# Encoder layer on one core: the third gate traced two products later, plain weights behind h's splits, other tiles for the sums of h, and scratch placed ahead of its rings

## The chip, the cores and the metric

The kernel runs on one core of a Trainium2 chip. The metric is the device time of one execution in microseconds (us). A profile of one execution is shown beside the times of several others.

## The reference

One layer of a hybrid encoder over 512 tokens of width 2048, in float32:

```python
h = rms_norm(x, pre_mix_g)
z = h @ w_in                                  # q, k, v (1024 each) and u (1024)
a = chunked_attention(q, k, v, rel_bias)      # 8 heads of 128, chunks of 64, 8 chunks back
p = multiscale_pool(u, pool_w, pool_scale)    # trailing means over 2, 4, 8, 16 tokens
x = x + rms_norm(concat(a, p) @ w_o, post_mix_g)
h = rms_norm(x, pre_ffn_g)
up = causal_dwconv(h @ w_up, conv_w, conv_b)  # w_up: 2048 x 11264, 3 taps
y = (gelu(up[:, :5632]) * up[:, 5632:]) @ w_down
x = x + rms_norm(y, post_ffn_g)
```

## The kernel before

**Products.** TensorE works on a rounded type, so each factor is split into a high part (rounded by ACT, L140) and a low part (the rest, subtracted by DVE, L141), and a product is the sum of two or three products of parts. The large products are also cut by a seven-product scheme: halves of both factors are added or subtracted, product i (1 to 7) is formed of such sums, and the results are combined. Products 5, 6 and 3 use sums of the left factor. Products 1, 6, 7 and 4 of a block add up in one PSUM bank (`qa`), 5 and 3 in another (`qg`), 2 in a third (`qd`). Products 6, 7 and 4 are "turned": the narrow matmuls with the low part (L176) come first, the wide ones with the high part (L170) second. One such product of the up projection is eight wide and eight narrow matmuls.

**Up projection.** It is done in 44 column blocks of 256 (block `PLAIN + k`; an even one feeds the gelu, the next odd one is multiplied by it). The first two blocks are plain (`plain`, three products of parts, no seven-product scheme); the other 42 are numbered k = 0 to 41. `Factors.order` is a hand-written order of pairs (k, i): the first eight are products 1 and 2 of blocks 0 to 3, then the plain blocks, then blocks 0 to 3 with spacing five, and from block 4 on with spacing seven. Around the places that matter here the order is

- (2,7), (3,3), (2,4), (3,6), (4,1), (3,7), (4,2), (3,4), (4,5), (4,3), (5,1), (4,6), ...
- at the end (41,5), (40,6), (41,3), (41,1), (40,7), (41,6), (40,4), (41,7), (41,2), (41,4).

`seven(k, i)` first calls `factors.get()`, which prepares the factor four products ahead (`AHEAD`): a split into two slots of the ring `w4` (eight slots, `wfh`, `wfl`), and behind it, on POOL, an accumulating load (L1110) that turns the raw block in place into the next sum that is needed. Then it issues the matmuls. `keep(k, i)` moves results out of PSUM: L1416 copies the bank of 5, L1421 the bank of 1, 6 after product 6, L1427 after 7. After product 4 `keep_all(k)` puts the block z together (L1435 to L1438). Then `gate(u, z)` (for even blocks) applies the three convolution taps (L1310 on ACT, L1311 and L1312 on DVE, for two halves) and the gelu (L1333) into the second half of the tile `zc`; `product(u, ...)` (odd blocks) applies the taps to its own z, multiplies into the same half (L1343), and stores the result to DRAM from it (L1346, POOL). z itself is the first half of `zc`.

**h.** Before that, h is transposed in eight pairs (`turn_back`; pairs 0 to 3 by `turn(0, 1)` and `turn(2, 3)`, the others between the groups of the first plain block) and split into the tiles `gT`. `h_sums` forms the sums for products 5, 6 and 3, each as two halves of 8 KB, in the tiles h0 to h5 of the pool `ps`, which held other data before.

**Down projection.** The seven-product scheme again, in five blocks of the inner dimension (CU = 4 up blocks each). Left factors (`ah`, `al`) are split from `gc` (loaded from DRAM) or from `s` in `scratch`; right factors (`bh`, `bl`) are split from `t` or `b`; for three of the first right factors the split lies ready in DRAM (`rw01`, `rw11`, `rw02`, each `h` and `l`) and is loaded by POOL (L1214). The first left factor `a` is split into two slots of `w4`. Two products with it come first (`pa`), then the product `pd` with `rw02` and the first `ah`. The pool `pr` lies over the tiles of `ps`: its `wh` and `wl` tiles take `rw01` and `rw11`. The pool `p4` lies over the pools of the up projection; its rings stand one behind the other in the order of the loop `for r in (...): r("place")`: among them `slot_h` (eight slots of 4 KB for `ah`), `slot_l` (eight for `al`) and `scratch` (one of 4 KB). In the version before, the first slot of `slot_h` lies exactly over the first slot of `w4`, `scratch` over the small tiles of the pool `p3`. A tile that lies over another is free to be written as soon as what used the other tile is done.

**Order.** TensorE's instructions stay in the order of the program. Those of the other engines are placed by a planner, which issues what it holds for ready and uses the place in the program as a priority. `tc.issue_after(ins)` adds an edge: what is traced in the block is issued behind `ins` on `ins`'s engine. Each engine then runs its own queue in order.

Of the kernel before, what the change touches and what calls it, by code (L numbers as in the profile page):

```python
# [81 lines left out]
def encoder_layer(ctx: ExitStack, tc: tile.TileContext, x, xT, vecs, rel, post_mix, post_ffn,  # L82
# [23 lines left out]
    def bank(name):  # L106
        return psum.tile([P, 512], F32, tag="ps", name=name)
# [30 lines left out]
    def split(hi, lo, src, scale=None):  # L138
        if scale is None:
            rounded = nc.scalar.activation(hi, src, AF.Copy)  # L140
            rest = nc.vector.tensor_sub(lo, src, f32(hi))  # L141
        else:
            rounded = nc.scalar.activation(hi, src, AF.Copy, scale=scale)
            rest = nc.vector.scalar_tensor_tensor(lo, src, scale, f32(hi), op0=ALU.mult, op1=ALU.subtract)
        split.last, split.rest = rounded.ins, rest.ins
        return rounded.ins
# [213 lines left out]
    for kb in range(KD):  # L360
        i, o = divmod(kb, 8)
# [259 lines left out]
    with tc.tile_pool(name="p1", bufs=2, reuse_waits="tile") as p1:  # L621
# [90 lines left out]
        def turn(h):  # L712
            probs = [state.pop(("p", h, t)) for t in range(NT)]
            pts = [bank(f"pt{h}_{k}") for k in range(3)]
            pts = [pts[0], pts[1][:, P:], pts[2][:, 2 * P:], pts[1][:, :P]]
            for k in (0, 1, 3, 2):
                for t in range(k, NT):
                    nc.tensor.transpose(pts[k][:, (t - k) * P:(t - k + 1) * P],
                                        probs[t][:, k * P:(k + 1) * P], ident)
            for k in range(NT):  # L720
                n, at = S - k * P, PT_AT[k] + k * P - PT_Q[k]
                split(pth[:, at:at + n], ptl[:, at:at + n], pts[k])
# [179 lines left out]
    if True:  # L902
# [56 lines left out]
        a22 = wo_left("a22", 1, 1, [acc8(f"a22{p}", "A", F32R).rearrange("p (a b) -> p a b", a=8) for p in "hl"])  # L959
# [189 lines left out]
        factors = Factors()  # L1149
# [33 lines left out]
    later, turns = {}, {}  # L1183
# [122 lines left out]
    if True:  # L1306
# [16 lines left out]
        def new_z():  # L1323
            return two(holder("zc")[0])

        def gate(u, z):
            if u == NU - 1:
                a = raw1("ca")[:, :2, :]
            else:
                a = two(holder("zc")[1])  # L1330
            for j in range(2):
                taps(z[:, j, :], 2 * u + j, a[:, j, :])
            nc.scalar.activation(flat(a), flat(a), AF.Gelu_apprx_tanh)  # L1333
            return a

        def product(u, g, z):
            for j in range(2):
                if u == NU - 1 and j:
                    c = raw_x("cx")[:, :S]
                else:  # L1340
                    c = holder("m8")[0]
                taps(z[:, j, :], KF + 2 * u + j, c)
                nc.vector.tensor_mul(g[:, j, :], g[:, j, :], c)  # L1343
            if u < NC * CU:
                for i in range(2):
                    nc.gpsimd.dma_start(gd[u // CU][i][:, u % CU, :, :], g[:, :, i * H:(i + 1) * H])  # L1346
            elif u < NU - 1:
                nc.gpsimd.dma_start(gd_last[u - NC * CU], g)
            else:
                product.last = g  # L1350
# [23 lines left out]
        def h_sums():  # L1374
            def keep(n, i, at, v):
                hs.setdefault(n, {})[i] = h8(at, f"h{n}{i}", F32R).rearrange("p (a b c) -> p a b c", a=4, b=2)
                split(*(hs[n][i][:, :, p, :] for p in range(2)), v)

            halves = [[wholes[k, t][:, 4 * i:4 * i + 4, :] for k in range(2) for t in range(2)] for i in range(2)]
            for i, (a11, a21, a12, a22) in enumerate(halves):  # L1380
                nc.vector.tensor_sub(a22, a22, a21)
                keep(5, i, (4, 1)[i], a22)
                nc.vector.tensor_sub(a21, a11, a21)
                nc.vector.scalar_tensor_tensor(a22, a22, -1.0, a11, op0=ALU.mult, op1=ALU.subtract)
                keep(6, i, (0, 5)[i], a22)
            for a11, a21, a12, a22 in halves:
                nc.vector.scalar_tensor_tensor(a12, a22, -1.0, a12, op0=ALU.mult, op1=ALU.subtract)
            for i in range(2):
                keep(3, i, (3, 2)[i], halves[i][2])
            return [v[1] for v in halves]  # L1390

        banks, gates = {}, {}

        zs = {}
# [7 lines left out]
        def keep(k, i):  # L1402

            if i == 1:
                v = zs[k, "1"] = first_parts[:, k % 4, :]
                nc.scalar.activation(v, banks[k, "a"][:, :T], AF.Copy)
                nc.vector.tensor_add(v, banks[k, "a"][:, T:], v)
            elif i == 2:
                v, d = zs[k, "1"], banks.pop((k, "d"))
                nc.vector.tensor_add(v, d[:, :T], v)  # L1410
                nc.vector.tensor_add(v, d[:, T:], v)
            elif i in (5, 3) and k < 4:
                return
            elif i == 5:
                zs[k, "5"] = raw_x("zb")[:, :S] if k == end else holder("m8")[1]
                nc.scalar.activation(zs[k, "5"], banks[k, "g"], AF.Copy)  # L1416
            elif i == 6:
                m = raw_x("zm") if k == end else holder("m8")[2]
                zs[k, "m"] = m.rearrange("p (a b c) -> p a b c", a=2, b=2)
                v = wide(zs[k, "m"][:, :1])  # L1420
                nc.scalar.activation(v, banks[k, "a"], AF.Copy)  # L1421
                nc.vector.tensor_add(v, banks[k, "g"] if k < 4 else banks.pop((k, "g")), v)
                if k < 4:
                    nc.vector.tensor_add(v, banks.pop((k, "e")), v)
            elif i == 7:
                v = wide(zs[k, "m"][:, 1:])
                nc.scalar.activation(v, banks[k, "a"], AF.Copy)  # L1427
                nc.vector.tensor_add(v, banks.pop((k, "g")) if k < 4 else zs.pop((k, "5")), v)
            elif i == 4:
                keep_all(k)  # L1430

        def keep_all(k):
            one, m, a = zs.pop((k, "1")), zs.pop((k, "m")), banks.pop((k, "a"))
            z = new_z()
            nc.scalar.activation(z[:, 0, :T], one, AF.Copy)  # L1435
            nc.vector.tensor_add(z[:, 1].rearrange("p (a b) -> p a b", a=2), m[:, :, 0], m[:, :, 1])
            nc.scalar.activation(z[:, 0, T:], a[:, T:], AF.Copy)
            nc.vector.tensor_add(z[:, 0, T:], a[:, :T], z[:, 0, T:])  # L1438
            u, p = divmod(PLAIN + k, 2)
            if p:  # L1440
                product(u, gates.pop(u), z)
            else:
                gates[u] = gate(u, z)

# [19 lines left out]
        def start(k, i):  # L1464
            seven(k, i)
            keep(k, i)
# [5 lines left out]
        for k, i in factors.order[:7]:  # L1472
            start(k, i)
        turn(0, 1)
        start(3, 2)
        turn(2, 3)
        factors.open = True
        def plain(p, behind):
            ups = [bank(f"up{p}_{j}") for j in range(2)]
            for q in range(4):  # L1480
                factors.used += 1
                factors.prefetch(0)
                factors.prefetch(factors.AHEAD if p else (2, 2, 3, factors.AHEAD)[q])
                w = weights.get(f"w{p}0_{q}", 0)
                for kb in range(4 * q, 4 * q + 4):
                    for j in range(2):
                        mm3(ups[j], part(w, j, slice(kb % 4 * P, (kb % 4 + 1) * P)), g_both(hT, kb),
                            kb == 0, kb == KD - 1)
                behind(q)
            return ups  # L1490
# [24 lines left out]
        for k, i in factors.order[8 + 4 * PLAIN:]:  # L1515
            seven(k, i)
            keep(k, i)
            if (k, i) == (end, 6):
                summed.close()
                pr = ctx.enter_context(tc.tile_pool(name="pr", bufs=2, side="right", reuse_waits="tile"))  # L1520
            if (k, i) == (end, 6):
                next_first()
            elif (k, i) == (end - 1, 4):
                next_first()
# [5 lines left out]
    with tc.tile_pool(name="p4", bufs=2, reuse_waits="tile") as p4:  # L1530
# [3 lines left out]
        raw2 = later["raw2"] = ring("raw2", (CU, S), 2)  # L1534
        half_g = ring("g", (CU, 2, H), 2)
        slot_h, slot_l = ring("ah", (CU, H), 8), ring("al", (CU, H), 8)
        scratch = ring("scratch", (CU, H), 1)
        product_part = later["part"] = ring("part", (2, S), 5)
# [2 lines left out]

        for r in (product_part, later["wh"], half_g, later["raw1"], raw2, later["wl"], slot_h, slot_l, scratch):
            r("place")
        half_g("place")
        for _ in range(3):
# [230 lines left out]
```

## Time and profile before

| | |
|---|---|
| times of three runs | 1865.05, 1865.7, 1866.84 us |
| median | 1865.7 us |
| profiled execution | 1864.49 us, span 1862.6 us |
| mean granted clock of TensorE | 0.998 |
| TensorE busy | 1840.5 us, 9514 matmuls |
| DVE, ACT, POOL busy | 1484.1, 1100.1, 306.8 us |

The span runs from the first to the last instruction of the profiled execution. A row of the timeline gives the start, the duration, the engine, the line in the kernel, the operation, what it writes and reads, and in square brackets how long the engine had been idle before it and what ended that. A row of the waits gives the engine and line that waited, what it waited for, the total in us, how often, and the longest. PE is TensorE.

### The profile page before, as it was taken

What the parts mean: (1) busy time and instruction counts of PE and PEld (TensorE: products, weight loads), DVE (VectorE), ACT (ScalarE), POOL (GpSimd) and SP (SyncE); (2) the same over time, 40 slices, a digit from 0 to 9 for tenths busy, and PEclk for the clock granted to TensorE, in tenths of its full rate; (3) what the DMA queues carried; (4) which work ended last, traced back from release to release, by engine and by line L of the source; (5) the groups of instructions that cost most, each with busy time, mean ns of one, the idle gap of its engine ahead of it and who ended that gap; (6) DMA issues with size and microseconds to landing.
All of it is one profiled execution on the core that took longest, in us unless ns stands there. A gap on an engine that the chain in (4) does not pass through costs nothing.

```text
span 1862.6 us, 25315 instructions
## 1 busy us (share of the span) xinstructions
PE 1840.5 (99%) x9514; PEld 1579.1 (85%) x9514; DVE 1484.1 (80%) x1776; ACT 1100.1 (59%) x1438; POOL 306.8 (16%) x407
## 2 busy tenths in 40 slices
PE   9999999999999989999999999999999999999998
PEld 7888888888888878888888888888888888888886
DVE  6988778888678777777787777777776899899876
ACT  7655455456586655665666665666655665565553
POOL 3411001100001212212212122121121001111101
PEclk9999999999999999999999999999999999999999
DMA  8599977998979878998988888899888977777785
GB/s 319 176 317 300 323 228 228 271 275 313 328 270 293 200 172 192 206 208 199 200 201 206 207 200 199 202 206 204 203 177 280 354 228 173 196 207 179 175 241 148
DMA packets 139547, 428.63 MB, mean 230 GB/s; under 512 B 12001, under 2 KB 15457, under 8 KB 133729
## 3 DMA queue, kind: packets, MB, share of 16 engines
q0 software_dynamic: 55440, 175.66, 46.9%
q1 hardware_dynamic: 83984, 251.36, 38.2%
q8 instruction: 75, 1.23, 0.3%
q14 instruction: 48, 0.39, 0.1%
HBM read 372.97 MB, written 104.33 MB: 256 GB/s over the span
## 4 chain that ended last, share of the span: by engine, by line
PE 65%; DMA 2%; issue 1%; DVE 1%; ACT 0%; POOL 0%; POOLq 0%; DVEq 0%; ACTq 0%
PE qa L170 15%; PE qa L176 8%; PE qg L170 8%; PE qg L176 4%; PE pa L162 4%; PE pa L164 4%; PE pa L165 4%; PE qd L170 4%; PE pg L162 2%; PE pg L164 2%; PE pg L165 2%; PE qd L176 2%; DMA bl<-rw02l 1%; PE pd L164 1%; PE pd L165 1%
## 5 line engine op out<-in xcount | busy, mean ns | idle before, releaser
L170 PE MATMUL qa<-gT,wfh 128*128 128x512 f32 x1176 | 294.6, 392 | 0.0
L141 DVE TENSOR_TENSOR wfl<-x,wfh 128x1024 fp32r<-128x1024 f32 x161 | 197.2, 1225 | 88.3 <-ACT wfh L140 83.8
L170 PEld LDWEIGHTS qa<-gT,wfh 128*128 128x128 f32 x1176 | 211.6, 189 | 37.9
L140 ACT ACTIVATE wfh<-x 128x1024 fp32r<-128x1024 f32 x161 | 170.3, 1058 | 97.4 <-PE qg L170 47.2
L1110 POOL DMA_DIRECT2D x<-in_w_up x122 | 104.7, 858 | 462.8 <-DVE wfl L141 438.3
L176 PE MATMUL qa<-gT,wfl 128*128 128x256 f32 x1176 | 164.7, 283 | 2.2 <-ACT m L1421 2.1
L170 PE MATMUL qg<-h,wfh 128*128 128x512 f32 x640 | 159.5, 392 | 5.5 <-ACT m L1416 5.5
L176 PEld LDWEIGHTS qa<-gT,wfl 128*128 128x128 f32 x1176 | 154.7, 191 | 6.8 <-ACT m L1421 2.3
L170 PEld LDWEIGHTS qg<-h,wfh 128*128 128x128 f32 x640 | 121.0, 189 | 30.9 <-ACT m L1416 5.7
L141 DVE TENSOR_TENSOR bl<-b,bh 128x2048 fp32r<-128x2048 f32 x56 | 127.2, 2288 | 18.6 <-ACT bh L140 11.7
L140 ACT ACTIVATE wfh<-wy 128x1024 fp32r<-128x1024 f32 x98 | 103.4, 1055 | 64.6 <-PE qd L170 49.0
L140 ACT ACTIVATE bh<-b 128x2048 fp32r<-128x2048 f32 x56 | 106.1, 1913 | 57.1 <-DVE b L1230 23.3
L141 DVE TENSOR_TENSOR wfl<-wy,wfh 128x1024 fp32r<-128x1024 f32 x98 | 119.5, 1219 | 10.5 <-ACT wfh L140 6.9
L162 PE MATMUL pa<-bh,ah 128*128 128x512 f32 x320 | 124.5, 389 | 0.0
L164 PE MATMUL pa<-bl,ah 128*128 128x512 f32 x320 | 124.5, 389 | 0.0
L165 PE MATMUL pa<-bh,al 128*128 128x512 f32 x320 | 124.5, 389 | 0.0
L170 PE MATMUL qd<-gT,wfh 128*128 128x512 f32 x392 | 97.0, 390 | 0.0
L176 PEld LDWEIGHTS qg<-h,wfl 128*128 128x128 f32 x640 | 87.3, 190 | 6.2
L176 PE MATMUL qg<-h,wfl 128*128 128x256 f32 x640 | 89.2, 282 | 0.0
L170 PEld LDWEIGHTS qd<-gT,wfh 128*128 128x128 f32 x392 | 73.2, 188 | 15.0
L170 PE MATMUL qa<-h,wfh 128*128 128x512 f32 x336 | 84.1, 392 | 0.0
L141 DVE TENSOR_TENSOR wfl<-wz,wfh 128x1024 fp32r<-128x1024 f32 x49 | 60.0, 1224 | 28.5 <-PE qa L170 25.3
(574 smaller groups left out, 4340.6 us busy)
## 6 DMA issues: line engine op xcount, KB each, us to landing
x<-in_w_up POOLq DMA_DIRECT2D x122, 512.0 KB, 5.9
b<-in_w_down SPq DMA_DIRECT2D x32, 1024.0 KB, 6.8
wt<-in_w_o POOLq DMA_DIRECT2D x24, 1024.0 KB, 14.7
wz<-in_w_up SPq DMA_DIRECT2D x42, 512.0 KB, 5.1
x<-in_w_up SPq DMA_DIRECT2D x42, 512.0 KB, 5.0
wy<-in_w_up SPq DMA_DIRECT2D x42, 512.0 KB, 3.8
wy<-in_w_up POOLq DMA_DIRECT2D x42, 512.0 KB, 6.0
sum<-part POOLq DMA_DIRECT2D x38, 512.0 KB, 6.2
```

Of the source, the lines that this page charges most:

```text
L140: rounded = nc.scalar.activation(hi, src, AF.Copy)
L141: rest = nc.vector.tensor_sub(lo, src, f32(hi))
L162: nc.tensor.matmul(ps, l[0], r[0], start=first, stop=False, skip_group_check=onto)
L164: nc.tensor.matmul(low, l[0], r[1], start=False, stop=False, skip_group_check=onto)
L165: nc.tensor.matmul(ps, l[1], r[0], start=False, stop=last, skip_group_check=onto)
L170: nc.tensor.matmul(ps, w[0][:, kb], pairs[kb][0], start=fresh and not kb, stop=last, skip_group_check=not fresh)
L176: nc.tensor.matmul(ps[:, sl], w[1][:, kb], pair[:, sl], start=False, stop=last, skip_group_check=not fresh)
L1110: nc.gpsimd.dma_start(self.raw[k, what], self.block(k, m, kh), accum_op=ALU.add)
```

## The change

- In `h_sums` the halves of sum 5 go to h1 and h0 (before: h4 and h1), the first half of sum 6 to h4 (before: h0). The second half of sum 6 and sum 3 stay.
- `keep_all(2)` no longer calls `gate` for block 2 (u = 2, the third gate). It keeps u and z, and the loop calls `gate` after product (4,1) and its `keep`, two products after (2,4).
- In the first plain block the factor preparation is cut from two ahead to one in the first group, and what is prepared in the first two groups gets edges behind the splits of h after `turn(0, 1)` and `turn(2, 3)`, on ACT and on DVE.
- In `p4` `scratch` is placed ahead of `slot_h` and `slot_l`, so both rings lie 4 KB further on.

```diff
-                keep(5, i, (4, 1)[i], a22)
+                keep(5, i, (1, 0)[i], a22)
 ...
-                keep(6, i, (0, 5)[i], a22)
+                keep(6, i, (4, 5)[i], a22)
 ...
             if p:
                 product(u, gates.pop(u), z)
+            elif k == 2:
+                zs["late"] = u, z
             else:
                 gates[u] = gate(u, z)
 ...
         turn(0, 1)
+        behind_h = [(split.last, split.rest)]
         start(3, 2)
         turn(2, 3)
+        behind_h.append((split.last, split.rest))
 ...
                 factors.prefetch(0)
-                factors.prefetch(factors.AHEAD if p else (2, 2, 3, factors.AHEAD)[q])
+                with ExitStack() as behind_split:
+                    for ins in behind_h[q] if not p and q < 2 else ():
+                        behind_split.enter_context(tc.issue_after(ins))
+                    factors.prefetch(factors.AHEAD if p else (1, 2, 3, factors.AHEAD)[q])
 ...
             keep(k, i)
+            if (k, i) == (4, 1):
+                u, z = zs.pop("late")
+                gates[u] = gate(u, z)
 ...
-        for r in (product_part, later["wh"], half_g, later["raw1"], raw2, later["wl"], slot_h, slot_l, scratch):
+        for r in (product_part, later["wh"], half_g, later["raw1"], raw2, later["wl"], scratch, slot_h, slot_l):
             r("place")
```

## The prediction

> **What bounds the kernel now.** First the page and the waits of TensorE, to see how much can be won at all.
>
> ```profile
> span 1862.6 us, 25315 instructions
> PE 1840.5 (99%) x9514; PEld 1579.1 (85%) x9514; DVE 1484.1 (80%) x1776; ACT 1100.1 (59%) x1438; POOL 306.8 (16%) x407
> ...
> PE qg L170 <- ACT m L1416: 5.5, 1, 5.5
> PE qa L176 <- ACT m L1421: 2.1, 1, 2.1
> PE up L164 <- DVE gT L141: 1.6, 1, 1.6
> PE pd L164 <- DMA bl<-rw02l: 1.5, 1, 1.5
> PE pd L162 <- ACT ah L140: 1.1, 1, 1.1
> ```
>
> TensorE is busy for 99% of the span, and no matmul is added or removed. What the change can win is the list of waits. The first five rows come to 11.8 us and sit at three places, near 575, 673 to 692, and 1438 us; each part of the change lies ahead of one of them. So I read the three places in the timelines of the engines. The profiled execution took 1864.49 us, 1.9 around its span; the median shown, 1865.7, is 1.2 above it. A TensorE gap that closes comes off either one whole.
>
> **Plain weights behind h's splits.** The view is the timeline: start, duration, engine, line, idle time and what ended it.
>
> ```profile
> 573.01 0.48 PE L162 MATMUL up<-gT,w_0h 128*128 128x512 f32 x1
> 575.05 0.51 PE L164 MATMUL up<-gT,w_0h 128*128 128x512 f32 x1 [1.56 <-DVE gT L141]
> 581.20 0.48 PE L162 MATMUL up<-gT,w_1h 128*128 128x512 f32 x1
> 570.47 1.08 ACT L140 ACTIVATE w_2h<-w_2r 128x1024 fp32r<-128x1024 f32 x1
> 571.42 1.07 ACT L140 ACTIVATE gT<-a 128x1024 fp32r<-128x1024 f32 x1
> 571.50 1.22 DVE L141 TENSOR_TENSOR w_1l<-w_1r,w_1h 128x1024 fp32r<-128x1024 f32 x1
> 572.63 1.22 DVE L141 TENSOR_TENSOR w_2l<-w_2r,w_2h 128x1024 fp32r<-128x1024 f32 x1
> 573.77 1.22 DVE L141 TENSOR_TENSOR gT<-a,gT 128x1024 fp32r<-128x1024 f32 x1
> ```
>
> The second matmul of plain product 0 needs the low half of gT, whose subtraction stands behind w_1l and w_2l on DVE and whose rounding stands behind w_2h on ACT. The issue_after edges force the opposite order on both engines. ACT then rounds gT at 570.5 instead of 571.4 and is done by 571.5; DVE is free at 571.50 and finishes the low half at 572.8. TensorE asks for it at 575.05 - 1.56 = 573.5. The wait goes: 1.56 us. What is pushed back is w_1l, to about 572.8 to 574.0, and w_2 and w_3, to behind the second split, about 579. w_1 is first read at 581.20, w_2 and w_3 later still, so their cover is 7 us. Queues: the next weights' loads on SP wait for raw slots that free up to 4 us later. They are for the second plain product, sixteen matmul groups on, so I cost that at nothing. Bounds: 0 (the planner puts other DVE work into the hole) to 1.56; I take 1.56, because an edge, unlike a priority, cannot be jumped.
>
> **The third gate.**
>
> ```profile
> 675.46 1.21 PE L176 MATMUL qa<-gT,wfl 128*128 128x256 f32 x8 [2.13 <-ACT m L1421]
> 684.25 1.98 PE L170 MATMUL qg<-h,wfh 128*128 128x512 f32 x8
> 692.71 3.41 PE L170 MATMUL qg<-h,wfh 128*128 128x512 f32 x8 [5.54 <-ACT m L1416]
> 673.41 1.52 ACT L1310 ACTIVATE zc<-zc,vec 128x512 f32<-128x512 f32 x2 [3.58 <-DMA gd<-zc]
> 674.83 0.58 ACT L1421 ACTIVATE m<-qa 128x512 f32<-128x512 f32 x1
> 676.90 0.42 ACT L1435 ACTIVATE zc<-first_parts 128x256 f32<-128x256 f32 x1 [0.54 <-DVE zc L1312]
> 677.22 0.36 ACT L1406 ACTIVATE first_parts<-qa 128x256 f32<-128x256 f32 x1
> 687.74 1.06 ACT L140 ACTIVATE wfh<-x 128x1024 fp32r<-128x1024 f32 x1 [5.48 <-DMA x<-in_w_up]
> 674.25 0.75 DVE L1311 SCALAR_TENSOR_TENSOR zc<-zc,vec 128x511 f32<-128x511 f32 x1 [4.83 <-ACT zc L1310]
> 674.92 1.22 DVE L141 TENSOR_TENSOR wfl<-x,wfh 128x1024 fp32r<-128x1024 f32 x1
> 679.24 1.22 DVE L141 TENSOR_TENSOR wfl<-x,wfh 128x1024 fp32r<-128x1024 f32 x1
> 680.76 0.91 POOL L1110 DMA_DIRECT2D x<-in_w_up  x1 [13.19 <-DVE wfl L141]
> ```
>
> One stall makes both gaps. The gate's two taps (L1310) overwrite the tile that product 1 is still storing, so ACT stands 3.58 us for the store; L1421, queued behind them, holds up the matmuls at 675.46. DVE stands 4.83 us with it, the low half at 679.24 comes late, the accumulating load of x leaves POOL at 680.76, ACT waits 5.48 us for it and goes on at 687.74, 7.0 us after the issue, and L1416 (the copy of (4,5)'s bank), behind that, holds up product (4,3) until 692.71, another 4.97 us.
>
> Does tracing the gate later move the taps behind L1421? I think not. The planner places what is ready and uses the trace position only between ready ones: L1435 at 676.90 belongs to keep_all(3), traced after product (3,4), and stands ahead of L1406 at 677.22, which is traced three products earlier. And on DVE the first tap's L1311 stands ahead of the low half at 674.92, whose slot is free only when the last matmul of (3,6) has read it. So in the plan the first tap on ACT was over before (3,6) ended, when L1421 cannot have been ready. A later trace position does not hold it back, and the wait of 2.13 us stays.
>
> What does change is who goes first on DVE when several are ready. L1422, L1424 and the low half of (4,5) now outrank the gate's remaining taps. The second pair, L1311 and L1312 (0.67 us each from start to start, as between the DVE rows at 674.25 and 674.92), falls behind that low half, which starts 1.3 us earlier, and so do POOL's load, its landing, and (4,3). The gap shrinks from 5.54 to 4.2 us. The gelu comes up to 2.7 us later; the 5.48 us that ACT idles ahead of 687.74 hide it.
>
> The gap has a second price. Eight wide matmuls last 1.98 us at 684.25 and 3.41 after the gap, at 692.71: 1.43 us more. The stretches show why; the column after the engines is the granted clock.
>
> ```profile
> 675.50:678.50 3.00, 3.00 (x17) 2.67 (x18) 3.00 (x5) 1.55 (x3) 0.00 (x0) 1.00 0.39 102
> 687.20:692.70 5.50, 0.00 (x0) 0.00 (x0) 2.96 (x4) 3.57 (x5) 0.85 (x1) 0.95 0.89 154
> 692.70:695.70 3.00, 2.99 (x7) 2.39 (x8) 2.12 (x4) 1.23 (x2) 0.00 (x0) 0.53 0.97 193
> ```
>
> After the 2.13 us gap the clock is 1.00; after 5.54 it is 0.53. A mean of 0.95 over 5.5 idle us, if it fell to one half once, puts the fall 0.55 us before their end (0.05 x 5.5 / 0.5), 5.0 us after the last matmul. A gap of 4.2 us ends before that, so I take the 1.43 as saved too. Together 2.7 us; bounds 0 and 8.5 (2.13, all of 5.54 but the 0.6 that a copy like L1421 takes in any case, and 1.43).
>
> The Trainium skill, page "TensorE: Matmul & The Clock Gate", Part 1, says the clock goes to half after an idle window of about 3.4 us, counted by windows that run free of the kernel. By that rule read strictly, 4.2 us is still too long, the 1.43 us stays, and the whole sum below becomes 5.5 instead of 6.9, or 1860.2 us. The trace agrees on the half clock (0.53 after 5.54 us) and shows no gap between 2.13 and 5.54 us.
>
> **Tiles of h's sums, and scratch ahead of its rings.** These act together at the last change of stage.
>
> ```profile
> 1404.26 1.98 PE L170 MATMUL qg<-h,wfh 128*128 128x512 f32 x8
> 1438.76 0.49 PE L162 MATMUL pd<-bh,ah 128*128 128x512 f32 x1 [1.15 <-ACT ah L140]
> 1440.72 0.50 PE L164 MATMUL pd<-bl,ah 128*128 128x512 f32 x1 [1.48 <-DMA bl<-rw02l]
> 1437.65 1.06 ACT L140 ACTIVATE ah<-gc 128x1024 fp32r<-128x1024 f32 x1 [8.99 <-PE pa L165]
> 1406.04 0.86 POOL L1110 DMA_DIRECT2D x<-in_w_up  x1 [7.50 <-DVE wfl L141]
> 1414.97 0.55 POOL L1214 DMA_DIRECT2D bh<-rw01h  x1 [7.51 <-PE qa L170]
> x<-in_w_up POOLq DMA_DIRECT2D x1, 512.0 KB, 5.4
> bh<-rw01h POOLq DMA_DIRECT2D x1, 1024.0 KB, 5.7
> bl<-rw11l POOLq DMA_DIRECT2D x1, 1024.0 KB, 14.3
> bl<-rw02l POOLq DMA_DIRECT2D x1, 1024.0 KB, 18.7
> ```
>
> Six loads of 1 MB leave POOL, rw01, rw11 and rw02, each a high and a low half, the first four from 1414.97 on. The first lands in the first tile of the old sums, which held half of sum 6, read by (41,6) until then; the other three queue behind it. They land 5.7 to 14.3 us after issue, about 2.9 us per MB, and push rw02l, issued near 1422.0 (1440.7 less 18.7), to 1440.7. Now that tile holds half of sum 5, last read by (41,5), two products of 2.79 us before (41,3) and so over at 1401.5; the next load's tile held half of sum 3, read until (41,3), begun at 1404.26, ends at 1407. So rw01h leaves near 1402 and the other three near 1407.5, behind the x load of 1406.04. All four are in by about 1420, and rw02l lands at its own price and one MB more, 8.6 to 11.5 us (one or two MB at 2.9 us on top of 5.7), near 1432. TensorE asks for it at 1437.6, where its wait for ah begins. Moved past on POOL: the x load for (41,4). It lands 5.4 us after 1406.04, and the rounding of it is not due before the slot frees at about 1413.8, so 2 us are in hand.
>
> That alone leaves 1.15: ACT's rounding of ah stood 8.99 us for the last matmul on the first a. Its slot, the ring's first or second, lies over the low half of that a. With scratch ahead the rings start 4 KB later, so it lies over a factor of one of the last products ((41,7), four after (41,3), ends at 1421.0 and (41,4) at 1426.6), and the rounding follows the landing of gc instead. Scratch now lies on a's slot and is free from 1437.4; the product that needs it starts two products of 5.4 us after that, so that costs nothing. Either part alone leaves a gap (the slot alone the whole 2.6, the tiles alone about 1.1); together 2.63 goes. Bounds 0 and 2.63. What is late next is the factors of the following products, whose loads also land earlier. In h_sums itself the new tiles are free long before their writes: nothing.
>
> **Sum.** 1.56 + 2.7 + 2.63 = 6.9 us: 1864.5 less 6.9 is 1857.6 for the profiled execution, 1858.8 for the median.
>
> **Rivals.**
> - The gate does move behind L1421 and the low half of (4,5). For: the taps may be a near tie in the plan. Against: the two orders above. Then 2.13 goes; the low half follows (4,1)'s last read, 673.3, and the x load leaves at about 674.9; with the same 7.0 and 4.97 (4,3) starts at 686.9, where TensorE is free at 687.2 - 2.13 = 685.0: a gap of 1.9 and no half clock. 2.13 + 3.64 + 1.43 = 7.2 instead of 2.7: 11.4 in all, 1854.3.
> - The end or the plain weights give nothing because the planner fills the hole or picks another slot, or the gate gives nothing: 1860.4 to 1863, taken as 1861.7.
> - Slower: POOL takes the rw loads ahead of the x load of (41,4). Three MB at 2.9 us in front of it and 5.4 for itself from about 1409 put it at 1423.1; ACT's rounding (1.06) and L1421 (0.58) of (41,6) follow, and (41,7) starts at 1424.8 instead of 1418.2: 6.6 us, and 1.43 for the clock. 1865.7 + 8.0 - 6.9 = 1866.8; with only the end's 2.63 won beside it, 1871.1. It decides once that load lands after 1416.5. Against: it leaves at 1406.04, a microsecond before the second rw load's tile is free.
>
> **How the numbers follow.** Forecast 0.49 (1857.5 to 1860.5, the clock's 1.43 included), the moving gate 0.19, a part that gives nothing 0.22, slower 0.10. The predicted time is the forecast's, 1858.8. The range 1853.8 to 1863.5 takes in the moving gate and most of the failed parts, and leaves out about 2 in 10. 0.2% is 3.7 us, about what a measurement can tell here: faster needs less than 1862.0. Forecast and moving gate give that with nearly all of 0.68, the failed parts with a third: 0.74. Same 0.20, slower 0.06.
>
> **What would show it.** Right: no wait of up on gT; L1310 still ahead of L1421 with a wait for gd, the wait of qa near 2.1 and of qg near 4.2 at full clock; rw01h issued near 1402, no wait of pd on rw02l or ah. Wrong: L1310 behind L1421; rw01h still after 1414; a new TensorE wait between 1405 and 1425 on L1421, or after 1448 on the next factors.

## The result, and the profile after

The changed kernel takes 1857.36 us (median of 5 runs, 1855.83 to 1857.90), the kernel before 1866.84 us on the same chip (5 runs, 1865.05 to 1867.86). The ratio is 0.995, 95% interval 0.9935 to 0.9965, so the gain is 9.5 us, between 6.5 and 12.1. The forecast was 1858.8 us and a gain of 6.9. The profiled execution took 1857.87 us. Its span is 6.6 us shorter than that of the first profile of before.

The two longest waits of TensorE in the changed kernel (us in total, times, longest); its span is 1856.0 us.

```profile
PE qa L176 <- ACT m L1421: 3.1, 1, 3.1
PE qg L170 <- ACT m L1416: 1.2, 1, 1.2
```

Three of the five waits of before are gone: that of up on gT and the two of pd. The other two changed places in size: the one ahead of (3,7), on L1421, grew from 2.1 to 3.1 us, and the one ahead of (4,3), on L1416, fell from 5.5 to 1.2. Among the shorter waits one is new, 0.9 us for DVE at L742, near 346 us. It lies far ahead of what the change touches, and f0, the same kernel run again below, does not show it.

The timeline of the changed kernel at plain product 0, the stretch where the wait of 1.56 us stood:

```profile
573.49 0.47 PE L162 MATMUL up<-gT,w_0h 128*128 128x512 f32 x1
573.81 0.39 PE L164 MATMUL up<-gT,w_0h 128*128 128x512 f32 x1
571.14 1.06 ACT L140 ACTIVATE gT<-a 128x1024 fp32r<-128x1024 f32 x1
572.11 1.04 ACT L140 ACTIVATE w_1h<-w_1r 128x1024 fp32r<-128x1024 f32 x1
572.23 1.23 DVE L141 TENSOR_TENSOR gT<-a,gT 128x1024 fp32r<-128x1024 f32 x1
```

gT's rounding now stands ahead of w_1's on ACT, its low half is done at 573.46 (572.23 + 1.23), and the second matmul, at 573.81, follows the first with no idle time. The half is ready 0.35 us ahead, where the forecast had 0.7 (572.8 against 573.5).

The timeline of the changed kernel around the third gate:

```profile
675.20 2.08 PE L176 MATMUL qa<-gT,wfl 128*128 128x256 f32 x8 [3.08 <-ACT m L1421]
690.58 2.12 PE L170 MATMUL qg<-h,wfh 128*128 128x512 f32 x8 [1.22 <-ACT m L1416]
673.15 1.52 ACT L1310 ACTIVATE zc<-zc,vec 128x512 f32<-128x512 f32 x2 [4.53 <-DMA gd<-zc]
674.57 0.57 ACT L1421 ACTIVATE m<-qa 128x512 f32<-128x512 f32 x1
677.66 1.22 DVE L141 TENSOR_TENSOR wfl<-x,wfh 128x1024 fp32r<-128x1024 f32 x1
679.12 0.74 DVE L1311 SCALAR_TENSOR_TENSOR zc<-zc,vec 128x511 f32<-128x511 f32 x1
664.86 1.49 POOL L1346 DMA_DIRECT2D gd<-zc  x2 [1.01 <-DVE zc L1343]
679.18 0.91 POOL L1110 DMA_DIRECT2D x<-in_w_up  x1 [12.83 <-DVE wfl L141]
```

ACT still takes the taps (L1310) ahead of the copy L1421 and stands for the store of gd. On DVE the low half of (4,5) at 677.66 now stands ahead of the second tap pair. The load of x leaves POOL 6.03 us after the taps begin (679.18 - 673.15). Before it was 7.35 (680.76 - 673.41): 1.32 us less.

The same place by stretches; the clock is the number after the busy times of the engines.

```profile
670.99:674.40 3.41, 1.13 (x9) 0.90 (x7) 0.40 (x1) 1.25 (x2) 0.00 (x0) 1.00 0.49 199
674.40:677.81 3.41, 2.61 (x10) 2.51 (x11) 3.41 (x6) 2.54 (x6) 0.00 (x0) 0.50 0.24 65
677.81:681.23 3.42, 3.42 (x9) 2.65 (x9) 2.50 (x4) 1.29 (x2) 0.91 (x1) 0.50 0.36 108
```

The clock is at one half for 6.83 us, from 2.3 us into the gap ahead of (3,7) onwards. TensorE works 2.61 + 3.42 us of it, and at full speed that work takes half as long: 3.0 us lost, where the first profile of before lost 1.4 us behind its second gap.

The end, in the timeline of the changed kernel:

```profile
1402.62 0.86 POOL L1110 DMA_DIRECT2D x<-in_w_up  x1 [7.50 <-DVE wfl L141]
1403.91 0.67 POOL L1214 DMA_DIRECT2D bh<-rw01h  x1
1418.56 0.54 POOL L1214 DMA_DIRECT2D bl<-rw02l  x1
1430.51 1.06 ACT L140 ACTIVATE ah<-gc 128x1024 fp32r<-128x1024 f32 x1 [5.28 <-DMA gc<-gd]
1434.25 0.39 PE L164 MATMUL pd<-bl,ah 128*128 128x512 f32 x1
```

and the last load in its list of DMA issues (KB, us to landing):

```profile
bl<-rw02l POOLq DMA_DIRECT2D x1, 1024.0 KB, 14.0
```

rw01h leaves right behind the load of x, and ah's rounding follows the landing of gc, no longer the last matmul on a. rw02l lands at 1432.6 (1418.56 + 14.0), 1.7 us before its first reader.

### The profile page after: what moved, and what is told of

Its sections match the earlier page's. It is cut to its first block, busy times and chain, and to the rows that moved or that the text cites. A ratio compares the mean times of both kernels' runs of the same rounds, so it can differ in the third digit from the quotient of the medians.

```text
span 1856.0 us, 25317 instructions
## 1 busy us (share of the span) xinstructions
PE 1840.9 (99%) x9514; PEld 1580.5 (85%) x9514; DVE 1484.0 (80%) x1776; ACT 1099.0 (59%) x1438; POOL 306.5 (17%) x407
## 3 DMA queue, kind: packets, MB, share of 16 engines
q8 instruction: 75, 1.23, 0.3%
## 4 chain that ended last, share of the span: by engine, by line
PE 95%; DMA 2%; DVE 1%; issue 1%; ACT 0%; SPq 0%; POOL 0%; POOLq 0%; DVEq 0%; ACTq 0%
PE qa L170 19%; PE qa L176 10%; PE qg L170 9%; PE qd L170 5%; PE qg L176 5%; PE pa L165 4%; PE pa L164 4%; PE pa L162 4%; PE m L162 3%; PE m L164 3%; PE m L165 3%; PE qd L176 3%; PE pg L165 2%; PE pg L164 2%; PE pg L162 2%; PE v L164 2%
## 5 line engine op out<-in xcount | busy, mean ns | idle before, releaser
L165 PE MATMUL pa<-bh,al 128*128 128x512 f32 x320 | 124.5, 389 | 0.0
```

What stands on the lines that cost most here:

```text
L165: nc.tensor.matmul(ps, l[1], r[0], start=False, stop=last, skip_group_check=onto)
```

## The experiments

Twelve runs were made, in three sets, each set with the kernel before beside it (medians 1868.08, 1867.21 and 1867.31 us). A difference of one or two us is less than these comparisons tell apart, so the waits in the traces carry the readings, and the ratios say where they suffice.

### One part taken back at a time

**e1, the plain weights.** The edges go, and the old counts come back:

```diff
-                with ExitStack() as behind_split:
-                    for ins in behind_h[q] if not p and q < 2 else ():
-                        behind_split.enter_context(tc.issue_after(ins))
-                    factors.prefetch(factors.AHEAD if p else (1, 2, 3, factors.AHEAD)[q])
+                factors.prefetch(factors.AHEAD if p else (2, 2, 3, factors.AHEAD)[q])
```

> The changed kernel with the edges behind h's splits taken out and the earlier prefetch counts put back. Theory (the edges alone move gT's low half ahead): the wait of up for gT's low half on DVE is back at 1.5 to 1.6 us, the gate's region and the end stay as in the changed kernel, and the time is 1.5 us above the changed kernel's 1857.4, near 1858.9. Rival (the new order comes from the other parts' shifts in the plan): no such wait, and the changed kernel's time. On the clock, for this and the three other kernels of this set: if a gap past some length between 2.1 and 3.1 us always halves the clock, every gap of about 3.1 us ahead of product (3,7) is followed by half speed; if windows of 3.4 us that run freely decide, the same gap goes without it in some of the executions, and half speed lasts 3.4 or 6.8 us.

1858.66 us, ratio to before 0.9953 (0.994 to 0.9965). The wait is back at its size, in the timeline of e1:

```profile
575.52 0.50 PE L164 MATMUL up<-gT,w_0h 128*128 128x512 f32 x1 [1.57 <-DVE gT L141]
```

So the edges and the lower count remove it, and no other part does; this run takes both back and does not tell them apart. The clock fell at 677.25 in this run, just behind a gap of 3.11 us, and stayed low for 3.41 us, not 6.83.

**e2, the gate.** The lines that delay it go (`elif k == 2: zs["late"] = u, z`, and the call behind (4, 1)).

> The changed kernel with the third gate traced where it was before, right behind product (2,4). Theory (the place in the trace sets only who goes first on DVE): ACT's order is the same, the second tap pair on DVE stands ahead of the low half of (4,5) again, the load of x leaves POOL about 1.3 us later against TensorE, the gap ahead of (4,3) is back at 4 to 5.5 us and the one ahead of (3,7) at 2 to 3 us; the two gaps and the half clock together cost 1.4 to 2.7 us more than in the changed kernel, so 1858.8 to 1860.1. Rival (the gate part gave nothing, since the first gap grew by what the second lost): within 0.7 us of the changed kernel's 1857.4.

1860.94 us, ratio 0.996 (0.9947 to 0.9973). The waits of e2:

```profile
PE qg L170 <- ACT m L1416: 3.8, 1, 3.8
PE qa L176 <- ACT m L1421: 3.8, 1, 3.8
```

and its timeline:

```profile
675.37 1.52 ACT L1310 ACTIVATE zc<-zc,vec 128x512 f32<-128x512 f32 x2 [5.21 <-DMA gd<-zc]
676.80 0.57 ACT L1421 ACTIVATE m<-qa 128x512 f32<-128x512 f32 x1
679.94 0.74 DVE L1312 SCALAR_TENSOR_TENSOR zc<-zc,vec 128x510 f32<-128x510 f32 x1
681.20 1.21 DVE L141 TENSOR_TENSOR wfl<-x,wfh 128x1024 fp32r<-128x1024 f32 x1
682.72 0.91 POOL L1110 DMA_DIRECT2D x<-in_w_up  x1 [14.83 <-DVE wfl L141]
```

The order on ACT is the same, both tap pairs stand ahead of the low half again, and the load of x leaves 7.35 us after the taps, as before the change. Both gaps are followed by half clock, 3.4 us each. The two gaps and the clock cost 3.76 + 3.85 + 3.4 = 11.0 us, against 3.08 + 1.22 + 3.0 = 7.3 in the changed kernel. The mechanism is as said. By these two traces the part is worth 3.7 us, more than the 1.4 to 2.7 expected; by the ratios it is 1.9, with intervals that overlap. And the first gap is not the 2.13 of the first profile.

**e3, the tiles of h's sums.** `(1, 0)[i]` and `(4, 5)[i]` become `(4, 1)[i]` and `(0, 5)[i]` again.

> The changed kernel with the tiles of the sums 5 and 6 of h put back. Theory: rw01h leaves POOL at about 1408 to 1410 (some 7 us before 1414.97, taken back, less what the kernel is ahead by) only after (41,6) has read half of sum 6, rw02l lands late again, and TensorE waits for it at pd: a gap of about 1.5 us, with the wait for ah gone because its slot still lies over a factor. Time 1858.9. Rival (the slots set both waits): no wait at pd, 1857.4.

1861.83 us, ratio 0.9972 (0.9961 to 0.9983), the largest loss of the four. Timeline of e3:

```profile
1433.21 0.50 PE L162 MATMUL pd<-bh,ah 128*128 128x512 f32 x1 [0.45 <-ACT ah L140]
1435.62 0.50 PE L164 MATMUL pd<-bl,ah 128*128 128x512 f32 x1 [1.91 <-DMA bl<-rw02l]
```

Its list of DMA issues, and the stretch behind these gaps:

```profile
bl<-rw02l POOLq DMA_DIRECT2D x1, 1024.0 KB, 18.4
```

```profile
1436.40:1439.82 3.42, 3.42 (x9) 2.64 (x8) 1.86 (x2) 2.30 (x3) 0.00 (x0) 0.50 0.70 293
```

rw01h left POOL at 1410.13, 6.2 us later than in the changed kernel, and rw02l took 18.4 us, where it had taken 18.7 before the change. The gaps come to 2.36 us, where 1.5 were expected, and a stretch at half clock follows them: 1.7 us more (3.42 busy us at half speed). No wait for ah was expected. The one of 0.45 us has another end than before: ACT, at 1432.10, had stood 8.30 us for the landing of gc, not for a matmul on a.

**e4, the scratch.** In the order of placing, `scratch` goes behind `slot_h, slot_l` again.

> The changed kernel with scratch behind the rings again. Theory: ah lies over the low half of the first a again, ACT's rounding of it waits for the last matmul on that a (idle about 8 to 9 us with TensorE as its end), and TensorE waits 1.1 us at pd for ah; rw02l has landed by then. Time 1858.5 (the prediction's sentence that the slot alone leaves the whole 2.6 is about the other half and stands for e3). Rival (with the loads early the factor of ah has a second slot free): no wait, 1857.4.

1860.53 us, ratio 0.9962 (0.9949 to 0.9976). Timeline of e4:

```profile
1434.47 0.50 PE L162 MATMUL pd<-bh,ah 128*128 128x512 f32 x1 [1.15 <-ACT ah L140]
1435.73 0.50 PE L165 MATMUL pd<-bh,al 128*128 128x512 f32 x1 [0.53 <-DVE al L141]
1433.36 1.06 ACT L140 ACTIVATE ah<-gc 128x1024 fp32r<-128x1024 f32 x1 [8.99 <-PE pa L165]
```

ACT stood 8.99 us for the last matmul on a, as before the change. The wait for ah is back, and one of 0.53 us for the low half behind it, which before lay under the wait for rw02l: 1.68 us, where 1.1 were expected.

### What holds the two gaps of the gate's region

**f0** is the changed kernel again, the yardstick of its set.

> The changed kernel itself, as the yardstick of this set. Theory of free windows for the clock: the waits are again 3.1 and 1.2 us, but where the clock falls against the gap, and whether it stays low for one window of 3.41 us or two, is another draw; so the time moves by up to 3 us between executions. Rival (a gap of 3.1 us always does the same): the fall comes 2.3 us into the gap again and lasts 6.8 us.

1857.21 us, ratio 0.9944 (0.993 to 0.9957). Waits of 3.32 and 1.22 us. The clock fell at 673.95, 1.95 us into the gap, and stayed low for 6.83 us. That is nearly the same draw as the first profile and decides nothing alone; e1 and e3, with the same code in this region, lost one stretch of 3.41 us.

**f1 and f2**, edges that put the gate behind the copy of (3,6), and in f2 behind the rounding of (4,5) as well:

```diff
-                nc.scalar.activation(v, banks[k, "a"], AF.Copy)
+                copied[k] = nc.scalar.activation(v, banks[k, "a"], AF.Copy).ins
...
-                gates[u] = gate(u, z)
+                with tc.issue_after(copied[3]):                              # f1
+                with tc.issue_after(copied[3]), tc.issue_after(split.last):  # f2
+                    gates[u] = gate(u, z)
```

> The changed kernel with one edge: the late gate is issued behind the copy of (3,6)'s bank (L1421). Theory (the first gap is ACT standing in the taps for the store of gd, with that copy queued behind): the copy runs 2 us before product (3,7) is due, the gap of 3.1 us and its half clock (1.7 to 3.0 us) go, and the gap ahead of (4,3) stays at 1 to 2 us since the rounding of (4,5) still stands behind the taps: 4.5 to 6 us off the changed kernel, 1851 to 1853 where it takes 1857.4. Rival (the stall only moves on, as it did from the second gap to the first): the gap ahead of (4,3) grows to 3 to 4.5 us with its own half clock, and the time is within 2 us of the changed kernel's.

> As the last, with the gate also behind the rounding of (4,5)'s high half on ACT. Theory: that rounding is then done at about 673, a microsecond after (4,1)'s last read, the low half follows, the load of x leaves POOL near 675, and the gap ahead of (4,3) falls to the copy's own 0.6 to 0.8 us: another 0.5 to 1 us off, 1850.5 to 1852. Rival (the late gelu or taps now hold up keep_all(3), the product or the roundings behind them): a new wait of TensorE between 683 and 700.

f1 takes 1856.65 us, ratio 0.9944 (0.9931 to 0.9956): no gain that the comparison can tell from f0. Its timeline:

```profile
669.04 0.60 ACT L1421 ACTIVATE m<-qa 128x512 f32<-128x512 f32 x1 [0.78 <-PE qa L170]
678.54 1.22 PE L176 MATMUL qa<-gT,wfl 128*128 128x256 f32 x8 [1.21 <-ACT m L1427]
687.25 3.59 PE L170 MATMUL qg<-h,wfh 128*128 128x512 f32 x8 [2.89 <-ACT m L1416]
```

The copy L1421 runs at 669.04 and the first gap is gone, so ACT standing in the taps was its cause. But the rival had the time right: the stall moved on, to the copy of (3,7) (L1427, behind an ACT instruction that stood for DVE's taps) and to (4,3), where 2.89 us are followed by half clock.

f2 takes 1852.29 us, ratio 0.9923 (0.9909 to 0.9936), where 1850.5 to 1852 were expected. The interval just touches that of f0. No wait on L1421 or L1427 is left. The one ahead of (4,3), from the timeline of f2, was expected at 0.6 to 0.8 us:

```profile
688.28 2.11 PE L170 MATMUL qg<-h,wfh 128*128 128x512 f32 x8 [1.39 <-ACT m L1416]
```

**f3, the gate traced two products later still**, behind (4,2): `if (k, i) == (4, 2):`.

> The changed kernel with the third gate traced two products later still, behind (4,2). Theory (the place in the trace sets only who goes first on DVE): ACT still takes the taps ahead of the copy L1421 and stands for the store of gd; first gap 3 us, second 1 to 2 us, the changed kernel's time within a microsecond or the clock's 1.3. Rival (two products were just too few): the taps fall behind L1421, the first gap goes, and the time falls by 4 us or more.

1857.65 us, ratio 0.9951 (0.9938 to 0.9964), the changed kernel's time. In its timeline the taps still stand ahead of the copy:

```profile
672.66 1.52 ACT L1310 ACTIVATE zc<-zc,vec 128x512 f32<-128x512 f32 x2 [3.54 <-DMA gd<-zc]
674.08 0.57 ACT L1421 ACTIVATE m<-qa 128x512 f32<-128x512 f32 x1
```

The place in the trace does not hold the taps back; the rival is out. The load of x leaves 6.03 us after the taps here too (678.69 - 672.66), so two products more give no more of the DVE effect. The first gap is 2.09 us here, where 3 were expected, since the store of gd let the taps go 7.2 us after its issue, and not 8.3 as in the changed kernel (664.86 to 673.15). In all ten profiles with the taps ahead of the copy and nothing filled into the gap, the gap is that time less 5.1 to 5.2 us (7.33 and 2.13 in before, 9.06 and 3.85 in g2): its size goes with the store, not with the place in the trace.

**h2, the taps of the product behind the copy of (4,5) too.** To f2 is added that the product of u = 2 is traced behind (4, 5) with an edge on L1416's instruction.

> The kernel with the gate behind the copy of (3,6) and the rounding of (4,5), and the taps of the product that uses the gate put behind the copy of (4,5) as well (L1416). Theory (the gap ahead of (4,3) is now set by ACT's order and no longer by the landing of x): the gap falls from 1.2 to 1.4 us to the copy's own 0.6 to 0.8 us and the time by 0.6 us, 1851.5 to 1852. Rival (the load of x still sets it): 1.2 us or more remain.

1851.27 us, ratio 0.9912 (0.9898 to 0.9926), the fastest kernel of the study. Its interval lies below that of f0. Timeline of h2:

```profile
682.12 1.06 ACT L140 ACTIVATE wfh<-wz 128x1024 fp32r<-128x1024 f32 x1 [1.43 <-PE qg L170]
683.09 0.58 ACT L1416 ACTIVATE m<-qg 128x512 f32<-128x512 f32 x1
683.72 2.12 PE L170 MATMUL qg<-h,wfh 128*128 128x512 f32 x8 [0.69 <-ACT m L1416]
```

With the taps out of the way the gap is 0.69 us, about the copy's own time (0.58). So what f2 had left ahead of (4,3) was the order on ACT, not the landing of x.

### The clock, and the kernel before again

**h1, the gap filled.** Seven matmuls on zeros, into a bank that nothing reads, behind product (4,1).

> The changed kernel with seven idle matmuls of 128 by 128 on zeros, into a bank that nothing reads, issued into the gap ahead of product (3,7). Theory (half clock follows a window idle for more than about half): they fill 1.5 us of the gap, at most 1.8 us of any window is idle, the copy L1421 comes no earlier, and the two windows at half clock go: 3.0 us off the changed kernel, or 1.5 to 1.7 where only one window was lost, about 1854.5. Rival (what matters is the time since the last needed matmul, or the throttle answers to something else than idleness): half clock as before and the changed kernel's time or more.

1856.76 us, ratio 0.9945 (0.9931 to 0.9958). The stretch of the gap in h1:

```profile
671.10:674.30 3.20, 1.75 (x16) 1.56 (x14) 1.18 (x2) 2.03 (x4) 0.00 (x0) 1.00 0.30 120
674.30:678.00 3.70, 3.68 (x20) 3.23 (x21) 3.70 (x6) 2.56 (x4) 0.00 (x0) 1.00 0.46 141
```

and its waits:

```profile
PE qa L177 <- ACT m L1422: 1.5, 1, 1.5
PE qa L177 <- ACT m L1428: 1.3, 1, 1.3
```

(The line numbers are one higher than in the changed kernel.) The gap still lasts 3.2 us, now half filled, and the half clock is gone: the granted clock is 0.999 in all five executions of h1, 0.997 to 0.998 in those of f0. So idleness is what the throttle answers to. But TensorE, at full clock behind the gap, now waits 1.3 us for the copy of (3,7), which it did not before. The span is 1.9 us shorter than f0's, not 3.0, and the runs show no difference.

**g1 and g2, the kernel before, profiled twice more.**

> The kernel before, profiled again, to see whether its first profile (1864.49 us, one window of half clock, 1.4 us) was a lucky draw: the medians put the gain of the change near 9.5 us and its steps explain 6.6. Theory (windows of 3.41 us that run freely, and a window idle for more than about half of it is followed by one at half clock): the waits are the same, the gap of 5.54 us always falls, and the gaps of 2.13 us and at pd (1.15 and 1.48 us) do so in about every second execution, at 1.5 us each; a profile with one of them more takes 1866 to 1868. Rival (the waits themselves differ between executions): the rows of waits move by a microsecond or more.

> As the last, another draw of the windows: the same rows of waits, and one, two or three stretches at half clock of 3.41 us or twice that, at places that the grid of the windows picks.

1867.02 and 1867.79 us. The waits of g1:

```profile
PE qg L170 <- ACT m L1416: 4.5, 2, 3.8
PE qa L176 <- ACT m L1421: 3.7, 1, 3.7
```

(the second wait on L1416, 0.75 us, lies near 1340 us, outside the gate's region) and its timeline:

```profile
666.43 1.50 POOL L1346 DMA_DIRECT2D gd<-zc  x2 [1.00 <-DVE zc L1343]
675.34 1.52 ACT L1310 ACTIVATE zc<-zc,vec 128x512 f32<-128x512 f32 x2 [5.15 <-DMA gd<-zc]
```

and a stretch of g2 at the end, behind the waits of pd:

```profile
1442.19:1445.61 3.42, 2.85 (x7) 2.27 (x8) 1.87 (x2) 3.42 (x4) 0.00 (x0) 0.50 1.02 428
```

Both theories are partly right. In g1 and g2 both gaps were followed by half clock, 3.4 us each, and in g2 the waits of pd as well. But the waits differ too: the first gap is 3.70 and 3.85 us, not 2.13, since the store of gd let the taps go 8.9 and 9.1 us after its issue, where the first profile shows 7.3 (666.08 to 673.41). The first profile of before was the lucky one: 9.1 us lost in the gate's region, against 10.9, 11.1 and 11.0 in g1, g2 and e2.

## Why the prediction was right, step by step

- **Plain weights, 1.56 us: right.** The wait went, e1 brings back 1.57, and nothing late came in its place.
- **The gate, 2.7 us: the mechanism right, the sizes not.** Right: the taps stay ahead of L1421 (after and f3), the second pair falls behind the low half of (4,5), and the load of x leaves 1.32 us sooner, forecast 1.3. Wrong were three sizes.
  - "The wait of 2.13 stays": that row was one draw of the store's landing. Without the gate's part it is 2.13, 3.70, 3.85 and 3.76 us (before, g1, g2, e2), with it 2.95 to 3.32 (after, f0, e1, e3, e4) and 2.09 in f3.
  - "The gap shrinks to 4.2": it shrank to 1.2 to 1.8. The step took the landing of 7.0 us from one row and counted on from there. Loads of x landed 5.7 to 5.8 us after issue in e1 and e3, and TensorE, slowed by the first gap and its half clock, came later. In the changed kernel, f0 and e4 ACT no longer stood for the load of x, and the order on ACT was the bound; in e1 and e3 it still stood 1.3 and 1.2 us for it, and their gaps are 1.8 and 1.7 us, not 1.2.
  - "At 4.2 us no half clock": the clock was judged by the length of the gap, and so it was in the strict reading beside it, but half clock came behind gaps of 2.1 us (f3) to 5.5 us, and not behind the 2.13 us of before. In the changed kernel it sits at the first gap and costs 1.7 to 3.0 us.
  The three errors cancel in good part, so that 2.7 came as near as it did was luck. Waits and clock together come to 7.3, 7.3, 6.6, 6.4 and 7.3 us in the five profiles with this part, 7.0 in the mean, and to 10.5 in the mean of the four without: 3.5 us for the 2.7 forecast. Of the 3.5, the second gap, the one that the forecast named, has 2.8, the clock 0.5 and the first gap 0.25, which by f3 is the store's doing and not the gate's.
- **Tiles and scratch, 2.63 us: right, with less in hand than said.** rw01h left behind the load of x and the store of gd, with the other three, where it was to leave five us ahead of them, and rw02l took 14.0 us for the 8.6 to 11.5 forecast. 1.7 us were left; by the forecast (1432 against 1437.6) it was 5.6. Of the prices of a part alone, the slot's held (2.6 forecast, 2.36 in e3), and the tiles' did not (1.1 forecast, 1.68 in e4), since the wait for al was missed.
- **The sum: near, and a little small in every term.** By the waits it is now 1.56 + 3.5 + 2.63 = 7.7 us, and about 0.5 more for the half clock behind pd, 1.4 us in one of three profiles of before: 8.2. The time between the starts of the same matmuls in the timelines takes in what the waits leave out: behind a wait a matmul lasts 0.50 us at first and not 0.39 (pd in before and after).

  | stretch of TensorE, us | without the part | with it | means apart |
  |---|---|---|---|
  | first plain matmul to (3,6) | 95.55, 95.60, 95.60, 95.60 (before, g1, g2, e1) | 93.86, 93.86 (after, f0) | 1.7 |
  | (3,6) to (5,1) | 28.35, 29.65, 29.91, 29.79 (before, g1, g2, e2) | 26.14, 26.10, 25.55, 25.31, 26.12 (after, f0, e1, e3, e4) | 3.6 |
  | (5,1) to the first of pa | 729.66, 730.71, 730.07 (before, g1, g2) | 729.66, 729.66 (after, f0) | 0.5 |
  | first of pa to the first L165 of pd | 14.49, 14.39, 14.50 (before, g1, g2) | 11.33, 11.33 (after, f0) | 3.1 |
  | from there to the last matmul | 413.34, 413.32, 414.41 (before, g1, g2) | 413.30, 413.30 (after, f0) | 0.4 |

  (3,6) and (5,1) stand for the first wide matmul of each. The three parts come to 8.8 us: 1.7 for 1.56, 3.6 for 2.7, and 3.5 (the last two rows) for 2.63. The 0.5 between lies where the change does nothing; it comes from short waits that vary between executions and that the first profile of before does not show, in g1 near 1340 us, in g2 near 1184. Ahead of the first plain matmul the three executions of the kernel before are 0.2 us quicker in the mean than these two of the changed one. Together 9.1, against 9.5 by the medians.
- **The rivals.** The gate does not move behind L1421. Had only the copy come free, it would not have brought the rival's 4.5 us over the forecast: f1 does that, and gains nothing over f0 that can be told. The rival moved the low half along with the copy; it takes f2's second edge for that, and f2 is 3.9 us below f0 by the ratios. The slower case did not come: the load of x left at 1402.62, ahead of the rw loads.

## What to carry to other kernels

Before a stall is priced, ask for the row of a second execution: a wait that a store ends was 2.13, 3.70 and 3.85 us in three executions of the kernel before, and the single profile here was the lucky one. A later place in a trace moves an instruction only among those that are ready; what kept the stalled instruction from blocking the copy behind it on ACT here was an explicit edge, and then the next instruction of that queue had to be looked at too (f1 gained nothing that could be told, f2 and h2 4 and 6 us by their ratios). Half clock is priced by how much of a window TensorE is idle, and what is saved of it may only meet the next wait.

## What the hardware showed

The clock goes by windows of 3.41 us that run freely. Every stretch at half clock amid the work lasted 3.41 or 6.83 us, wherever the gap lay, and the falls of one execution lie on one grid: in g2 those at 677.61 and 1442.19 are 224.0 windows of 3.413 us apart, in e3 those at 675.23 and 1436.40 are 223.0. The next rows are windows that end where the clock fell; the first number behind the length is TensorE's busy time. Of f3, 39% busy:

```profile
671.50:674.91 3.41, 1.32 (x10) 1.11 (x9) 1.41 (x2) 2.25 (x4) 0.00 (x0) 1.00 0.44 177
```

Of g2, 47% busy:

```profile
1438.78:1442.19 3.41, 1.61 (x6) 0.75 (x5) 1.18 (x1) 2.27 (x4) 0.00 (x0) 1.00 1.02 414
```

And one of the first profile of before, by the grid of its fall at 692.13 counted back, 49% busy, behind which the clock did not fall:

```profile
671.67:675.08 3.41, 1.66 (x12) 1.33 (x10) 0.83 (x2) 1.67 (x3) 0.00 (x0) 1.00 0.61 244
```

So a window busy for less than about half is followed by one at half clock, and a gap of 2.09 us (f3) was enough where it lay in one window. Counted so in all fourteen traces, each window at full clock that was busy for 47% or less was followed by half clock, and none of 49% or more was. At half clock, a window that was busy for 77% (after, 674.40 to 677.81) was followed by another at half clock, as was one of 60% (f0), and one of 83% (g2) by the full clock. The Trainium skill, page "TensorE: Matmul & The Clock Gate", Part 1, gives windows of 3413 ns that run free of the kernel, which these rows bear out, and says that the clock falls after an idle window; here a window 53% idle did it.

The store of gd, two of 256 KB, let the taps go between 7.2 us (f3) and 9.1 us (g2) after its issue, and in three executions of one kernel, the one before, 7.3, 8.9 and 9.1 us. Why is open.
